# Three direct hidden tiles instead of four in a hybrid decoder layer, and low weight halves made by adding transfers

## The chip, the cores and the metric

The kernel runs on one core of a Trainium2 chip. The metric is the device time of one execution in microseconds, the median of several runs. The core's engines each work through their own list of instructions in order: TensorE (PE, matmuls), VectorE (DVE), ScalarE (ACT), GpSimd (POOL) and SyncE (SP). They wait for one another through semaphores. Transfers are issued by an engine and then run by the DMA engines.

## The reference, cut to what matters

One decoder layer on x of 512 tokens and 1024 channels, all in float32: a feed-forward network (FFN1), a mixing stage of attention, convolution and memory attention, and a second feed-forward network (FFN2).

```
D_MODEL = 1024
SEQ = 512
D_FF = 256 * math.ceil(8 * D_MODEL / 3 / 256)      # 2816
...
def rms_norm(x, g):
    xf = x.astype(jnp.float32)
    y = xf * lax.rsqrt(jnp.mean(xf * xf, axis=-1, keepdims=True) + EPS)
    return (y * g.astype(jnp.float32)).astype(x.dtype)
...
def swiglu(x, w_gate, w_up, w_down):
    return (jax.nn.silu(x @ w_gate) * (x @ w_up)) @ w_down
...
        x = x + 0.5 * swiglu(rms_norm(x, g_ffn1[l]), w_ffn1_gate[l], w_ffn1_up[l], w_ffn1_down[l])
...
        x = x + jnp.concatenate([y_attn, y_conv, y_mem], axis=-1) @ w_out[l]

        x = x + 0.5 * swiglu(rms_norm(x, g_ffn2[l]), w_ffn2_gate[l], w_ffn2_up[l], w_ffn2_down[l])
```

## The kernel before

Tokens lie along the free axis (512 columns) and channels on the partitions, so x is 8 tiles of 128x512 in SBUF. Every operand of a matmul is split in two: a high half, which is the value cast to the type fp32r, and a low half, the value minus its high half. A product is then three matmuls, high by high, high by low and low by high (`mm3`, lines 350 to 352).

**A feed-forward network** has 22 hidden tiles f of 128 channels. The first four (`N_DIRECT`) are direct: gate and up are each 8 products of 512 columns, 48 matmuls for the tile. Their matmuls read xh and xl, the split x times the gain; the factor of the norm (rb, one number per token, spread over the partitions at line 395) is multiplied in afterwards by VectorE (`evac`, lines 413 to 417). The other 18 tiles are fast (`fast`): a block scheme with seven block products in place of eight, each 4 x 3 matmuls of 256 columns (lines 447 to 449), 84 for the tile. The fast tiles need x with the factor already in it and its block sums; `blocks(k)` makes these for channel tiles k and k + 4 (lines 426 to 440), on VectorE and ScalarE. There are four calls of it, one after each direct tile but the first, and one with tile 0's evacuation. `hidden` (lines 405 and 406) splits a finished hidden tile into hh and hl.

The down projection runs in rounds over groups of hidden tiles (`ROUNDS`): each round adds its share to all eight output tiles d of x. Round 0 stands directly after the direct tiles. In it, ScalarE copies the first four outputs from PSUM with the factor 0.5 and GpSimd adds them into x by an adding transfer (lines 505 and 506); VectorE adds the others (line 509). Later rounds are mixed in among the fast tiles, one load of weights at a time. The last round feeds what follows: `nxt.add` sums the squares of x for the next norm and `scaled_split` makes the next xh and xl.

**Weights** go through one list (`Weights`): SyncE loads raw float32 weights into four raw buffers, ScalarE casts the high half (line 170) and VectorE subtracts the low half (line 171). High and low lie in one of four weight buffers, taken in rotation, so the cast for an item waits until TensorE has read the item four places earlier; and a load waits until the raw buffer four places earlier has been read. Loads run three items ahead, conversions three items ahead.

**Order.** The order of instructions on each engine is arranged by a scheduler when the kernel is built, within what the tiles allow. On TensorE FFN2's first tile stands right behind the last matmuls of the mixing stage, which read the last weights of `wout_c` (their rows are named yh and yl).

Of the kernel before, what the change touches and what calls it, by code (L numbers as in the profile page):

```python
# [30 lines left out]
F32 = mybir.dt.float32  # L31
# [3 lines left out]
AF = mybir.ActivationFunctionType  # L35
ALU = mybir.AluOpType
# [4 lines left out]
KT = 8  # L41
NF = 22
# [31 lines left out]
TILES = [s[1:] for s in ORDER if s[0] == "p"]  # L74

ON_DVE = [(0,), (1, 3), (1, 3), (2, 3), (1, 3), (1, 3)]
ROUNDS = [(0, 4), (4, 8), (8, 12), (12, 16), (16, 18), (18, 22)]
N_DIRECT = 4
WIDE, HALF, OTHER, TURNED = 64, 140, 128, 244
N_ACT = 20  # L80

# [5 lines left out]
class Weights:  # L87
# [5 lines left out]
    def __init__(self, nc, pool, dma_ahead, conv_ahead, bufs):  # L93
        self.nc, self.pool = nc, pool
        self.dma_ahead, self.conv_ahead, self.bufs = dma_ahead, conv_ahead, bufs
        self.loads, self.items = [], []
        self.raw, self.after, self.split, self.piece = {}, {}, {}, {}
        self.sums = {}
        self.extra = None
        self.by_hand = 2  # L100
        self.loaded = self.done = self.at = self.turn = 0

    def add(self, ap, off=WIDE):

        self.loads.append(ap)
        i = len(self.loads) - 1
        self.items.append((i, int(np.prod(ap.shape[1:])), off, lambda: self.raw[i]))
# [13 lines left out]
    def make_sums(self, i):  # L121
# [8 lines left out]
        nc.vector.tensor_tensor(s43[:, r], g[:, l], u[:, l], op=ALU.add)  # L130
        self.sums[i] = (s12, s43)

    def load_to(self, n):
        while self.loaded < min(n, len(self.loads)):
            i = self.loaded
            ap = self.loads[i]
            raw = self.pool.tile([P, 1024], F32, tag="wraw", name=f"wraw{i}", bufs=self.bufs[0])
            self.raw[i] = raw
            if i >= self.by_hand:
                to = raw[:, : int(np.prod(ap.shape[1:]))]  # L140
                if len(ap.shape) == 3:
                    to = to.rearrange("p (a b) -> p a b", a=ap.shape[1])
                self.nc.sync.dma_start(to, ap)
            self.loaded += 1

    def split_to(self, n):
        nc = self.nc
        while self.done < min(n, len(self.items)):
            i = self.done
            need, cols, off, src = self.items[i]  # L150
            self.load_to(need + 1)
            if need in self.after:
                self.after.pop(need)()
            if off is None:
                c = (HALF - 128) // 4
                hi, lo = (
                    self.extra.tile([P, cols + 64], F32R, tag=t, name=f"{t}{i}", bufs=1)[:, c : c + cols] for t in ("vhi", "vlo")
                )
            else:

                j = self.turn % self.bufs[1]
                c = off // 4
                self.turn += 1
                both = self.pool.tile([P, 2048 + 64], F32R, tag=f"w{j}", name=f"w{i}", bufs=1)
                hi, lo = both[:, c : c + 1024], both[:, c + 1024 : c + 2048]
            if i < self.by_hand:
                self.piece[i] = (src(), hi, lo)
            else:
                raw = src()
                nc.scalar.copy(hi[:, :cols], raw[:, :cols])  # L170
                nc.vector.tensor_tensor(lo[:, :cols], raw[:, :cols], hi[:, :cols].bitcast(F32), op=ALU.subtract)  # L171
            self.split[i] = (hi, lo)
            self.done += 1
            if i >= self.by_hand:
                self.load_to(need + 1 + self.dma_ahead)
# [9 lines left out]
    def next(self):  # L185
        i = self.at
        self.at += 1
        self.split_to(i + 1 + self.conv_ahead)
        return self.split.pop(i)


def per_load(r):

    return 8 // (ROUNDS[r][1] - ROUNDS[r][0])


def steps(f):

    r = next(r for r, (lo, hi) in enumerate(ROUNDS) if lo <= f < hi)
    if r == 0:  # L200
        return [], [], []
    m = KT // per_load(0)
    if r == 1:
        i = f - ROUNDS[1][0]
        return [(0, g) for g in range(m - 1)] if i == 0 else [], [(0, m - 1)] if i == 1 else [], []

    queue = [(q, g) for q in range(1, len(ROUNDS) - 1) for g in range(KT // per_load(q))]
    return [], [queue[f - ROUNDS[2][0]]], []


def layer(tc, ctx, a):
    nc = tc.nc
    PE, ACT, DVE, POOL = nc.tensor, nc.scalar, nc.vector, nc.gpsimd
# [28 lines left out]
    W = Weights(nc, wpool, dma_ahead=3, conv_ahead=3, bufs=(4, 4))  # L242

    def flat(w):
        return w.rearrange("p k m -> p (k m)")

    def ffn_weights(n, memory):
        gu = a[f"wgu{n}"]

        def down(r, g):  # L250
            lo, hi = ROUNDS[r]
            m = per_load(r)
            return a[f"wd{n}"][g * m : (g + 1) * m, :, lo:hi].rearrange("d p k m -> p d (k m)")

        for f in range(NF):
            pre, mid, post = steps(f)
            for d in pre:
                W.add(down(*d), OTHER if d[0] else WIDE)
            if f < N_DIRECT:
                W.add(flat(gu[f, 0]))  # L260
                W.add(flat(gu[f, 1]))
            else:
                W.add_pair(flat(gu[f, 0]), flat(gu[f, 1]), [(down(*d), OTHER if d[0] else WIDE) for d in mid])
            for d in post:
                W.add(down(*d), OTHER if d[0] else WIDE)
            if memory and f == MEM_F:
                for t in range(2):
                    W.add(flat(a["wmk"][t]), HALF)
                for c in range(2):
                    W.add(flat(a["wmv"][:, 4 * c : 4 * c + 4]), TURNED)  # L270
        r = len(ROUNDS) - 1
        for g in range(KT // per_load(r)):
            W.add(down(r, g), (HALF, OTHER)[g % 2])
# [48 lines left out]
    rb = keep.tile([P, T], F32, name="rb")  # L322
# [41 lines left out]
    class Norm:  # L364
# [5 lines left out]
        def add(self, d, engine=POOL):  # L370
            sq = work() if d else tmp.tile([P, T], F32, tag="sqsum", name=nm("sqsum"), bufs=1)
            ACT.activation(sq, x[:, d], AF.Square)
            if d == 0:
                self.sum = sq
            else:
                (engine if d < KT - 1 else DVE).tensor_tensor(self.sum, self.sum, sq, op=ALU.add)
# [13 lines left out]
        def spread(self):  # L390
            ps = tp_bank()
            for b in range(NB):
                s = slice(b * P, (b + 1) * P)
                PE.transpose(ps[:, s], self.bc[:, s], ident)
            DVE.tensor_copy(rb, ps)

    def ffn(pool, norm, first, gain, hooks, next_gain, last):
        h_hi = [None] * NF
# [4 lines left out]
        def hidden(f, t):  # L403
            h_hi[f], h_lo[f] = atile("hh"), atile("hl")
            ACT.copy(h_hi[f], t)
            DVE.tensor_tensor(h_lo[f], t, h_hi[f].bitcast(F32), op=ALU.subtract)  # L406
# [113 lines left out]
        raw = {}  # L520
        for f in range(NF):
            pre, mid, post = steps(f)
            for d in pre:
                for step in down(*d):
                    step()
            if f >= N_DIRECT:
                fast(f, mid)
            else:
                g, u = (sc_bank(), sc_bank()) if f % 3 == 2 else (mm_bank(), mm_bank())
                gh, gl = W.next()  # L530
                if f == 0:
                    uh, ul = W.next()
                    for ks in first:
                        mm3(g, gh, gl, ks, xhk, xlk, ks[0] == 0, ks[-1] == 7)
                        mm3(u, uh, ul, ks, xhk, xlk, ks[0] == 0, ks[-1] == 7)
                    norm.stats()
                    held = (g, u)
                else:
                    mm3(g, gh, gl, range(8), xhk, xlk, True, True)
                    if f == 1:  # L540
                        norm.spread()
                        raw[0] = evac(0, *held)
                        blocks(0)
                        hidden(0, raw[0])
                    uh, ul = W.next()
                    mm3(u, uh, ul, range(8), xhk, xlk, True, True)
                    raw[f] = evac(f, g, u)
                    if f == 1:
                        hidden(1, raw[1])
                    blocks(f)  # L550
                if f == N_DIRECT - 1:
                    for i in range(2, N_DIRECT):
                        hidden(i, raw[i])
            for d in post:
                for step in down(*d):
                    step()
            for hook in hooks.get(f, ()):
                hook()
# [679 lines left out]
```

## Time and profile before

| what | value |
| --- | --- |
| median of 3 runs | 864.02 us (863.29 to 864.94) |
| the profiled execution's own time | 864.32 us |
| its span in the profile | 861.8 us |
| TensorE clock granted, mean | 0.998 |
| VectorE, 512 columns, line 417 | 684 ns each |
| VectorE, subtraction of 1024 columns, line 171 | 1224 ns each |
| ScalarE, cast of 1024 columns, line 170 | 1048 ns each |
| GpSimd's issue of an adding transfer, line 506 | 864 ns in the middle, 859 to 1211 |

The table's durations are those of single instructions; on one engine the next instruction can start before the last one's tail has ended, so the steps from start to start are a little shorter. A row of the timeline has the start in us, the duration in us, engine, line, operation, what it writes and reads (without buffer numbers), shape, and in brackets how long the engine had been idle and what ended that.

### The profile page before, as it was taken

To read this page: it belongs to the slowest core of one execution; us is meant where nothing else is said; L and a number is where in the kernel's file an instruction comes from. 1 tells how busy PE (TensorE), PEld (TensorE's weight loads), DVE (VectorE), ACT (ScalarE), POOL (GpSimd) and SP (SyncE) were. 2 spreads that over 40 slices of the span, in tenths; PEclk is the share of its full clock that TensorE was granted. 3 is DMA by queue.
4 is the path that set the end of the run, shared out by engine and by line. 5 is a ranking of instruction groups with operands and counts; after the bars stand their busy time and mean duration, and the time that the engine had idled before them with its cause. 6 is when DMAs were issued, how large, how long until landed. Compare 5 with 4: busy or idle time off the path is not lost.

```text
span 861.8 us, 15658 instructions
## 1 busy us (share of the span) xinstructions
PE 854.5 (99%) x6361; PEld 790.9 (92%) x6361; DVE 696.6 (81%) x1163; ACT 445.9 (52%) x741; POOL 27.4 (3%) x30
## 2 busy tenths in 40 slices
PE   8999999999999999999999999999999999999998
PEld 5889999999999999988776888889999999999998
DVE  7998987777868797869988985998887868687772
ACT  7455555455644454533948763454654545545540
POOL 0010000000000000300000021010000000000000
PEclk9999999999999999999999999999999999999999
DMA  7335334243553334222010322335334343333312
GB/s 274 122 97 152 100 101 129 86 127 119 141 163 104 122 110 129 82 90 62 19 43 14 116 93 93 102 87 159 99 98 124 98 123 95 109 92 115 107 49 99
DMA packets 34808, 91.44 MB, mean 106 GB/s; under 512 B 3248, under 2 KB 5808, under 8 KB 34736
## 3 DMA queue, kind: packets, MB, share of 16 engines
q1 hardware_dynamic: 32000, 85.99, 32.0%
q0 software_dynamic: 1584, 2.88, 2.0%
q10 hardware_dynamic: 1152, 1.57, 0.6%
q8 instruction: 50, 0.82, 0.4%
q14 instruction: 22, 0.18, 0.1%
HBM read 85.45 MB, written 2.10 MB: 102 GB/s over the span
## 4 chain that ended last, share of the span: by engine, by line
PE 97%; DVE 1%; ACT 1%; DMA 1%; issue 0%; SPq 0%; ACTq 0%; DVEq 0%
PE mm L350 16%; PE mm L352 15%; PE mm L351 15%; PE mm L449 11%; PE mm L448 11%; PE mm L447 11%; PE sc L449 2%; PE sc L448 2%; PE sc L447 2%; PE tp L951 1%; PE sc L352 1%; PE sc L350 1%; PE sc L351 1%; PE sc L880 1%; PE tp L965 1%; PE mm L880 1%
## 5 line engine op out<-in xcount | busy, mean ns | idle before, releaser
L447 PE MATMUL mm<-bh,w 128*128 128x256 f32 x864 | 238.8, 276 | 0.0
L448 PE MATMUL mm<-bl,w 128*128 128x256 f32 x864 | 238.6, 276 | 0.0
L449 PE MATMUL mm<-bh,w 128*128 128x256 f32 x864 | 238.6, 276 | 0.0
L351 PE MATMUL mm<-hl,w 128*128 128x256 f32 (+1 forms) x640 | 183.7, 288 | 0.0
L352 PE MATMUL mm<-hh,w 128*128 128x256 f32 (+1 forms) x640 | 183.6, 287 | 0.0
L350 PE MATMUL mm<-hh,w 128*128 128x256 f32 (+1 forms) x640 | 183.1, 287 | 0.0
L170 ACT CAST w<-wraw 128x1024 fp32r<-128x1024 f32 (+2 forms) x122 | 124.0, 1020 | 86.1 <-PE mm L352 25.1
L171 DVE TENSOR_TENSOR w<-wraw,w 128x1024 fp32r<-128x1024 f32 (+2 forms) x122 | 144.5, 1189 | 28.4 <-ACT w L170 23.1
L447 PEld LDWEIGHTS mm<-bh,w 128*128 128x128 f32 x864 | 162.2, 188 | 0.2
L448 PEld LDWEIGHTS mm<-bl,w 128*128 128x128 f32 x864 | 162.2, 188 | 0.1
L449 PEld LDWEIGHTS mm<-bh,w 128*128 128x128 f32 x864 | 162.2, 188 | 0.0
L351 PEld LDWEIGHTS mm<-hl,w 128*128 128x128 f32 x640 | 120.1, 188 | 2.6 <-DVE hl L406 0.2
L352 PEld LDWEIGHTS mm<-hh,w 128*128 128x128 f32 x640 | 120.2, 188 | 2.5
L350 PEld LDWEIGHTS mm<-hh,w 128*128 128x128 f32 x640 | 120.1, 188 | 2.4
L171 DVE TENSOR_TENSOR w<-s,w 128x1024 fp32r<-128x1024 f32 x72 | 88.0, 1223 | 41.5 <-PE mm L449 34.6
L170 ACT CAST w<-s 128x1024 fp32r<-128x1024 f32 x72 | 75.7, 1051 | 24.8 <-PE mm L449 20.4
L350 PE MATMUL mm<-xh,w 128*128 128x512 f32 x192 | 75.8, 399 | 0.6 <-ACT w L182 0.6
L351 PE MATMUL mm<-xl,w 128*128 128x512 f32 x192 | 75.6, 394 | 0.6 <-DVE xl L362 0.5
L352 PE MATMUL mm<-xh,w 128*128 128x512 f32 x192 | 75.3, 392 | 0.0
L509 DVE SCALAR_TENSOR_TENSOR x<-mm,x 128x512 f32<-128x512 f32 x80 | 54.0, 683 | 1.8 <-PE mm L352 1.8
L468 ACT ACTIVATE t<-t 128x512 f32<-128x512 f32 x36 | 22.8, 633 | 61.7 <-DVE t L467 61.7
L127 DVE TENSOR_TENSOR s<-wraw 128x512 f32<-128x512 f32 x36 | 24.9, 691 | 28.8 <-DMA wraw<-in_wgu 28.6
(244 smaller groups left out, 1370.5 us busy)
## 6 DMA issues: line engine op xcount, KB each, us to landing
wraw<-in_wgu SPq DMA_DIRECT2D x86, 512.0 KB, 3.6
wraw<-in_wd SPq DMA_DIRECT2D x44, 512.0 KB, 3.6
wraw<-in_win SPq DMA_DIRECT2D x12, 512.0 KB, 3.5
x<-t POOLq DMA_DIRECT2D x8, 256.0 KB, 4.5
out<-t SPq DMA_DIRECT2D x7, 256.0 KB, 2.0
x<-in_xT SPq DMA_DIRECT2D x3, 512.0 KB, 6.3
wraw<-in_wout_a SPq DMA_DIRECT2D x6, 256.0 KB, 2.6
wraw<-in_wgu SPq DMA_DIRECT2D x4, 256.0 KB, 4.7
```

What stands on the lines that cost most here:

```text
L127: nc.vector.tensor_tensor(s12[:, l], u[:, l], u[:, r], op=ALU.add)
L170: nc.scalar.copy(hi[:, :cols], raw[:, :cols])
L171: nc.vector.tensor_tensor(lo[:, :cols], raw[:, :cols], hi[:, :cols].bitcast(F32), op=ALU.subtract)
L350: PE.matmul(ps[:, t], wh[:, w], hi(k)[:, t], start=one, stop=False, skip_group_check=cut > 1)
L351: PE.matmul(ps[:, t], wh[:, w], lo(k)[:, t], start=False, stop=False, skip_group_check=cut > 1)
L352: PE.matmul(ps[:, t], wl[:, w], hi(k)[:, t], start=False, stop=end, skip_group_check=cut > 1)
L447: PE.matmul(ps, wh[:, c], bh[k][:, block], start=one, stop=False, skip_group_check=not first)
L448: PE.matmul(ps, wh[:, c], bl[k][:, block], start=False, stop=False, skip_group_check=not first)
L449: PE.matmul(ps, wl[:, c], bh[k][:, block], start=False, stop=end, skip_group_check=not first)
L468: ACT.activation(g, g, AF.Silu)
L509: DVE.scalar_tensor_tensor(o, ps, 0.5, xd, op0=ALU.mult, op1=ALU.add)
L880: PE.matmul(banks[h][:, i * ML + c.start : i * ML + c.stop], self.q[rows, n * P : (n + 1) * P], self.kt[rows, ks], start=True, stop=True, ...
```

## The change

Direct tiles are three instead of four in both networks, and the rounds become groups of 3, 4, 4, 4, 4 and 3 hidden tiles. Round 0 now has four loads of 768 columns (two outputs with three tiles each), all listed ahead of the first fast tile; the middle rounds have one load more than there are fast tiles to take them, and it comes behind the last one. The fourth call of `blocks` stands with the third direct tile. `hidden` follows each direct tile at once. ScalarE, no longer VectorE, copies the factor rb.

Some weights, marked `by_queue`, get their low half in another way: ScalarE writes the negated high half into the place of the low half, and GpSimd then issues an adding transfer which reads the same weights from HBM once more and adds them there. So marked are tile 2 in FFN1, tiles 0, 1 and 2 in FFN2 (gate and up each), and round 0's four loads in both: 16 transfers. VectorE's subtraction is left out for these.

```diff
-ROUNDS = [(0, 4), (4, 8), (8, 12), (12, 16), (16, 18), (18, 22)]
-N_DIRECT = 4
+ROUNDS = [(0, 3), (3, 7), (7, 11), (11, 15), (15, 19), (19, 22)]
+N_DIRECT = 3
...
-    def add(self, ap, off=WIDE):
-
+    def add(self, ap, off=WIDE, by_queue=False):
+
+        if by_queue:
+            self.by_queue.add(len(self.items))
...
+    @staticmethod
+    def shaped(to, ap):
+        to = to[:, : int(np.prod(ap.shape[1:]))]
+        return to.rearrange("p (a b) -> p a b", a=ap.shape[1]) if len(ap.shape) == 3 else to
...
                 raw = src()
                 nc.scalar.copy(hi[:, :cols], raw[:, :cols])
-                nc.vector.tensor_tensor(lo[:, :cols], raw[:, :cols], hi[:, :cols].bitcast(F32), op=ALU.subtract)
+                if i in self.by_queue:
+                    nc.scalar.activation(lo[:, :cols], hi[:, :cols].bitcast(F32), AF.Copy, scale=-1.0)
+                    nc.gpsimd.dma_start(self.shaped(lo, self.loads[need]), self.loads[need], accum_op=ALU.add)
+                else:
+                    nc.vector.tensor_tensor(lo[:, :cols], raw[:, :cols], hi[:, :cols].bitcast(F32), op=ALU.subtract)
...
-    m = KT // per_load(0)
     if r == 1:
-        i = f - ROUNDS[1][0]
-        return [(0, g) for g in range(m - 1)] if i == 0 else [], [(0, m - 1)] if i == 1 else [], []
+        return [(0, g) for g in range(KT // per_load(0))] if f == N_DIRECT else [], [], []
 
     queue = [(q, g) for q in range(1, len(ROUNDS) - 1) for g in range(KT // per_load(q))]
-    return [], [queue[f - ROUNDS[2][0]]], []
+    i = f - ROUNDS[2][0]
+    return [], [queue[i]], queue[i + 1 :] if f == NF - 1 else []
...
             for d in pre:
-                W.add(down(*d), OTHER if d[0] else WIDE)
+                W.add(down(*d), OTHER if d[0] else WIDE, d[0] == 0)
             if f < N_DIRECT:
-                W.add(flat(gu[f, 0]))
-                W.add(flat(gu[f, 1]))
+                for i in range(2):
+                    W.add(flat(gu[f, i]), WIDE, n == 2 or f > 1)
...
-            DVE.tensor_copy(rb, ps)
+            ACT.copy(rb, ps)
...
                     raw[f] = evac(f, g, u)
-                    if f == 1:
-                        hidden(1, raw[1])
+                    hidden(f, raw[f])
                     blocks(f)
                 if f == N_DIRECT - 1:
-                    for i in range(2, N_DIRECT):
-                        hidden(i, raw[i])
+                    blocks(f + 1)
```

The change moves instructions on all engines. Line numbers of the changed kernel are eight higher here (350 is 358, 395 is 403).

**VectorE at the norm's factor in FFN1.** w is a weight buffer, rb the factor, t and kept the two factors of tile 0's evacuation, braw the first blocks. Before:

```order
L386 COPY t_276<-rtok 128x512
L171 TENSOR_TENSOR w_339<-wraw_201,w_339 128x1024
L395 COPY rb<-tp_309 128x512
L413 TENSOR_TENSOR t_315<-mm_196,rb 128x512
L416 TENSOR_TENSOR kept_318<-mm_197,rb 128x512
```

In the changed kernel:

```order
L394 COPY t_277<-rtok 128x512
L421 TENSOR_TENSOR t_317<-mm_196,rb 128x512
L424 TENSOR_TENSOR kept_320<-mm_197,rb 128x512
L434 SCALAR_TENSOR_TENSOR braw_323<-x,par,rb 128x512
L425 TENSOR_TENSOR kept_320<-kept_320,t_317 128x512
```

The subtraction for a weight and the copy of rb are gone from VectorE, and the evacuation follows directly.

**TensorE at the start of round 0 in FFN1.** hh and hl are the split hidden tiles in the order of their numbers, mm the outputs, the third operand the weights of round 0. Before, with tiles 0, 1 and 2 (335, 374, 549) ahead of tile 3:

```order
L352 MATMUL mm_471<-xh_155,w_393 128x512
L350 MATMUL mm_562<-hh_335,w_422 128x512
L351 MATMUL mm_562<-hl_336,w_422 128x512
L352 MATMUL mm_562<-hh_335,w_422 128x512
L350 MATMUL mm_562<-hh_374,w_422 128x512
L351 MATMUL mm_562<-hl_375,w_422 128x512
L352 MATMUL mm_562<-hh_374,w_422 128x512
L350 MATMUL mm_562<-hh_549,w_422 128x512
```

In the changed kernel, at the end of the third bank's first part (tiles 0, 1 and 2 are 337, 377 and 462):

```order
L360 MATMUL mm_529<-hh_377,w_396 128x512
L358 MATMUL mm_498<-hh_462,w_341 128x512
L358 MATMUL mm_511<-hh_462,w_341 128x512
L358 MATMUL mm_529<-hh_462,w_396 128x512
L358 MATMUL mm_542<-hh_337,w_396 128x512
L359 MATMUL mm_542<-hl_338,w_396 128x512
L359 MATMUL mm_498<-hl_463,w_341 128x512
```

Three banks (498, 511 and 529) take their six matmuls of tiles 0 and 1 first, 18 in all, and then hh of tile 2; hl of tile 2 is read five matmuls after hh.

**ScalarE at the start of FFN2.** t is a square for the norm, xh the high half of x. Before, with w_5903 for tile 1's up weights and w_5822 for tile 0's:

```order
L372 ACTIVATE t_5852<-x 128x512
L361 ACTIVATE xh_5855<-x,par 128x512
L170 CAST w_5903<-wraw_5736 128x1024
L170 CAST w_5822<-wraw_5677 128x1024
L372 ACTIVATE t_5890<-x 128x512
L361 ACTIVATE xh_5893<-x,par 128x512
```

In the changed kernel (w_6002 for tile 1, w_5919 for tile 0):

```order
L380 ACTIVATE t_5950<-x 128x512
L369 ACTIVATE xh_5953<-x,par 128x512
L175 CAST w_6002<-wraw_5833 128x1024
L177 ACTIVATE w_6002<-w_6002 128x1024
L175 CAST w_5919<-wraw_5773 128x1024
L380 ACTIVATE t_5989<-x 128x512
L177 ACTIVATE w_5919<-w_5919 128x1024
L369 ACTIVATE xh_5992<-x,par 128x512
```

A negated copy (line 177) now stands behind each cast, and a square stands between the cast of w_5919 and its negated copy. On GpSimd the transfers follow in the same order, tile 1's ahead of tile 0's.

**TensorE at the same place.** mm_5901 and mm_5902 are gate and up of tile 0 before, and mm_5983 is the gate of tile 1. Before:

```order
L352 MATMUL mm_5901<-xh_5893,w_5733 128x512
L350 MATMUL mm_5902<-xh_5893,w_5822 128x512
L351 MATMUL mm_5902<-xl_5894,w_5822 128x512
L352 MATMUL mm_5902<-xh_5893,w_5822 128x512
L381 MATMUL tp_5961<-ones,sqsum_5745 128x1 x4
L350 MATMUL mm_5983<-xh_5747,w_5860 128x512
```

In the changed kernel (gate mm_6000 and up mm_6001 of tile 0, gate mm_6084 of tile 1):

```order
L358 MATMUL mm_6001<-xh_5844,w_5919 128x512
L359 MATMUL mm_6001<-xl_5845,w_5919 128x512
L358 MATMUL mm_6000<-xh_5992,w_5829 128x512
L359 MATMUL mm_6000<-xl_5993,w_5829 128x512
L360 MATMUL mm_6000<-xh_5992,w_5829 128x512
L389 MATMUL tp_6062<-ones,sqsum_5842 128x1 x4
L358 MATMUL mm_6084<-xh_5844,w_5958 128x512
L359 MATMUL mm_6084<-xl_5845,w_5958 128x512
L360 MATMUL mm_6084<-xh_5844,w_5958 128x512
L358 MATMUL mm_6084<-xh_5858,w_5958 128x512
L360 MATMUL mm_6001<-xh_5844,w_5919 128x512
L358 MATMUL mm_6001<-xh_5858,w_5919 128x512
```

The first 21 matmuls of tile 0's gate stand ahead of these rows. The statistics (line 389) and four matmuls of tile 1 are now ahead of the first matmul that reads the low half of w_5919 (line 360), and the other 21 matmuls of tile 0's up product stand behind it.

More of the change, by code (lines that the diff above doesn't have):

```diff
@@ L98, in __init__ @@
         self.sums = {}
+        self.by_queue = set()
         self.extra = None
@@ L139, in load_to @@
             if i >= self.by_hand:
[L140 to L143, printed above, removed]
+                self.nc.sync.dma_start(self.shaped(raw, ap), ap)
             self.loaded += 1
```

## The prediction, made before the changed kernel had run

> **What bounds the kernel now.** I read the page's busy times and its chain first, then what TensorE (PE) waits for, then single stretches of the timeline (start, duration, engine, line, operation, tiles).
>
> ```profile
> span 861.8 us, 15658 instructions
> PE 854.5 (99%) x6361; PEld 790.9 (92%) x6361; DVE 696.6 (81%) x1163; ACT 445.9 (52%) x741; POOL 27.4 (3%) x30
> ...
> PE 97%; DVE 1%; ACT 1%; DMA 1%; issue 0%; SPq 0%; ACTq 0%; DVEq 0%
> ```
>
> TensorE is busy for 854.5 of 861.8 us and holds 97% of the chain that ended last. So the time falls by what TensorE no longer computes, and rises by every wait that is put in front of it; VectorE (81%) and ScalarE (52%) count only where something of theirs comes late.
>
> ```profile
> PE tp L305 <- DVE pair L318: 1.2, 1, 1.2
> PE mm L350 <- ACT w L182: 0.6, 1, 0.6
> PE mm L351 <- DVE xl L362: 0.5, 1, 0.5
> ```
>
> These are TensorE's waits of the first 100 us (total, times, longest): 2.3 us, all in the opening, and none at a hidden tile. There is hardly any wait that an edit could remove.
>
> **Part 1: two hidden tiles go from direct to fast, one in each FFN.** In the rows L350 to L352 are the three matmuls of a product, and L447 is the first of the three in a fast tile.
>
> ```profile
> 42.01 0.39 PE L350 MATMUL mm<-xh,w 128*128 128x512 f32 x1
> ...
> 52.89 0.39 PE L350 MATMUL mm<-hh,w 128*128 128x512 f32 x1
> ...
> 69.28 0.28 PE L447 MATMUL mm<-bh,w 128*128 128x256 f32 x1
> ...
> 75.75 0.28 PE L447 MATMUL mm<-bh,w 128*128 128x256 f32 x1
> ```
>
> The first two rows bound the direct tile 3: 48 matmuls in 52.89 - 42.01 = 10.88 us, 0.2267 each. The last two lie 57 matmuls of 256 columns apart in a fast tile: 6.47 us, 0.1135 each; its 84 take 9.53. The difference is 1.35 us a tile, **-2.70 us** for two. The down products only change rounds: their number stays, and one of 512 columns (0.2267) costs what two of 256 do (0.2270).
>
> **Part 2: does VectorE keep up with an earlier round 0?** In FFN1 round 0 now starts at 42.01, after three direct tiles.
>
> ```profile
> 12.00:58.00 46.00, 45.52 (x206) 37.25 (x205) 43.95 (x73) 25.87 (x34) 0.00 (x0) 1.00 0.42 142
> ...
> 25.42 1.05 ACT L170 CAST w<-wraw 128x1024 fp32r<-128x1024 f32 x1 [3.94 <-DVE t L386]
> ...
> 26.50 1.23 DVE L171 TENSOR_TENSOR w<-wraw,w 128x1024 fp32r<-128x1024 f32 x1 [1.09 <-ACT w L170]
> 27.64 0.68 DVE L395 COPY rb<-tp 128x512 f32<-128x512 f32 x1
> 28.36 0.69 DVE L413 TENSOR_TENSOR t<-mm,rb 128x512 f32<-128x512 f32 x1
> 28.97 0.68 DVE L416 TENSOR_TENSOR kept<-mm,rb 128x512 f32<-128x512 f32 x1
> 29.57 0.74 DVE L426 SCALAR_TENSOR_TENSOR braw<-x,par,rb 128x512 f32<-128x512 f32 x1
> ```
>
> The first row has TensorE, its weight loads, VectorE and ScalarE busy in this stretch: VectorE 43.95 of 46.00, ScalarE 25.87. So VectorE is the tight one, and the change takes from it the copy of the factor rb and the subtractions for tile 2 and round 0, while ScalarE takes on a copy and the negated copies. In the rows, rb's copy stood behind the subtraction at 26.50, which waited for its cast. Copied by ScalarE it should be ready near 27.5, not 28.36.
>
> From there to the evacuation of tile 2's second product, VectorE has 26 instructions in the new order. I price them by steps from start to start: 0.60 for an operation on 512 columns (28.36 to 28.97 to 29.57) and 1.14 for 1024 (26.50 to 27.64), so about 1.07 for each further 1000 columns. By that line 256 columns are 0.335 and 768 are 0.87; a scalar_tensor_tensor (0.74 against 0.68) gets 0.66. 12 x 0.60 + 6 x 0.66 + 4 x 0.335 + 2 x 0.87 + 2 x 1.14 = 16.5, so that evacuation starts at 44.0. Two more steps and ScalarE's cast (0.62) give hh of tile 2 at 46.5. TensorE begins round 0 with the 18 matmuls of three banks that need only tiles 0 and 1: 42.01 + 18 x 0.2267 = 46.09. I take a wait of **+0.5**; the low half hl, used five matmuls later, comes at 47.7 and adds next to nothing. The least is 0. The most is 1.2: a cast for the first fast tile stands ahead of hh of tile 1 on ScalarE and waits for its load, worth 0.7 if that comes late. FFN2 copies rb with more slack, as its statistics move ahead of the second half of tile 0; there I take 0. The casts and subtractions for the first fast tile end by this ledger 0.5 to 2.8 us ahead of their matmuls (near 58.8), which is no cost but no comfort.
>
> **Part 3: the adding transfers.** There are 16 new ones: 6 in FFN1, 10 in FFN2. Each waits for a cast and a negated copy on ScalarE, then reads the weights from HBM a second time. The trace has adding transfers, of half the size.
>
> ```profile
> x<-t POOLq DMA_DIRECT2D x8, 256.0 KB, 4.5
> mtot<-t POOLq DMA_DIRECT2D x3, 256.0 KB, 5.2
> ...
> wraw<-in_wgu SPq DMA_DIRECT2D x86, 512.0 KB, 3.6
> ...
> DMA to landing us min/median/max: 3.4/4.5/7.8
> ...
> q1 hardware_dynamic: 32000, 85.99, 32.0%
> q0 software_dynamic: 1584, 2.88, 2.0%
> ```
>
> Eleven transfers of 256 KB make up q0: 0.020 x 861.8 / 11 = 1.57 us of all 16 DMA engines each. On q1 a MB takes 0.32 x 861.8 / 85.99 = 3.2 us, so 256 KB take 0.8: adding costs about twice a plain load. The bottom row of landing times is that of the eight into x: 3.4 at least, 4.5 in the middle, 7.8 at most. A second 256 KB adds 1.57: I estimate 5.0, 6.1 and 9.4 us for 512 KB. The lowest bound is 3.6, what a plain load of that size takes.
>
> ```profile
> 19.48 2.00 ACT L170 CAST w<-wraw 128x1024 fp32r<-128x1024 f32 x2 [1.23 <-PE mm L352]
> ...
> 31.13 0.39 PE L350 MATMUL sc<-xh,w 128*128 128x512 f32 x1
> ...
> 509.25 1.03 ACT L170 CAST w<-wraw 128x1024 fp32r<-128x1024 f32 x1
> ```
>
> Where there is lead, this hides. In FFN1 the pair of casts at 19.48 is tile 2's; the gate's negated copy follows, and its transfer issues near 22.4 to land from 27.4 to 31.8, where TensorE wants it two matmuls into tile 2, at 31.6. The last piece of round 0 can be cast when tile 2 ends (42.01), issues near 43.9, lands by 53.3 at worst, and is wanted two matmuls into the seventh of eight outputs: 42.01 + 0.5 + 56 x 0.2267 = 55.2. FFN2's gate weights for tile 0 are cast at 509.25, issue near 512 and are wanted two matmuls after 522.36, beyond the 9.4. What TensorE computes meanwhile is the cover.
>
> **The place without lead is FFN2's first up weights.** Their buffer is the one from which the last matmuls of the mixing stage read.
>
> ```profile
> 522.13 0.39 PE L352 MATMUL mm<-yh,w 128*128 128x512 f32 x1
> 522.36 0.39 PE L350 MATMUL mm<-xh,w 128*128 128x512 f32 x1
> ...
> 533.24 0.95 PE L381 MATMUL tp<-ones,sqsum 128*128 128x1 f32 x8
> 534.05 0.49 PE L350 MATMUL mm<-xh,w 128*128 128x512 f32 x1
> ...
> 521.02 0.71 ACT L361 ACTIVATE xh<-x,par 128x512 fp32r<-128x512 f32 x1
> 521.64 1.98 ACT L170 CAST w<-wraw 128x1024 fp32r<-128x1024 f32 x2
> 524.94 0.64 ACT L372 ACTIVATE t<-x 128x512 f32<-128x512 f32 x1 [1.32 <-DVE x L1132]
> 525.48 0.71 ACT L361 ACTIVATE xh<-x,par 128x512 fp32r<-128x512 f32 x1
> ...
> 523.03 1.21 DVE L171 TENSOR_TENSOR w<-wraw,w 128x1024 fp32r<-128x1024 f32 x1
> 524.17 0.68 DVE L1132 TENSOR_TENSOR x<-mm,x 128x512 f32<-128x512 f32 x1
> 524.77 1.21 DVE L171 TENSOR_TENSOR w<-wraw,w 128x1024 fp32r<-128x1024 f32 x1
> ```
>
> Mixing's last matmul starts at 522.13 and ends near 522.5. Before, ScalarE cast both the second tile's and these weights from 521.64 on, and VectorE had the low half at 526, in good time. Now the same half goes this way: the second tile's cast and negated copy hold ScalarE until 523.55 (521.64 + 2 x 0.95, since two took 1.98 with the last one's tail); the cast of w_5919 runs to 524.5, a square to 525.0 (0.53, from 524.94 to 525.48), its negated copy to 526.0; then GpSimd issues the transfer, near 526.0. No row has a negated copy; I price it as a cast of the same size, and even at half of that the landing moves by half a microsecond. Before the first matmul that reads this half TensorE has 26 matmuls of tile 0, the statistics (534.05 - 533.24 = 0.81) and 4 matmuls of tile 1: 522.36 + 30 x 0.2267 + 0.81 = 529.97. All later work of TensorE stands behind it, and nothing else can go ahead.
>
> Landing, and so the wait: with 3.6 us 529.6, no wait; with 5.0, 531.0 and 1.0; with 6.1, 532.1 and 2.1; with 9.4, 535.4 and 5.4. This one is not alone: tile 1's adding transfer of 512 KB was issued 2.4 us ahead on the same queue, and the cast of w_5919 frees the raw buffer for which three weight loads (512, 384 and 384 KB, by the rate above 4 us of all engines) stand in SyncE's queue, just then. All three transfers together are 2 x 3.14 + 4.0 = 10.3 us of work from about 525 on: 535.3 if this half is the very last of it, 531.3 if the loads yield. I take the middle, landing near 533.4: **+3.4 us**, from 0 to 5.4.
>
> A rule speaks against that. The Trainium skill, "DMA: Bandwidth & Descriptors", section "Anatomy of one DMA — SWDGE (gpsimd) path", fits a GpSimd transfer as 2.0 us plus its bytes over 436e3 per us, an estimate of 3.2 us for 512 KB: landing at 529.2, no wait, and a sum of 861.8. The same fit gives 2.6 us for 256 KB, which took 3.4 to 7.8 here, so the trace does not agree.
>
> **Sum.** -2.70 + 0.5 + 3.4 = +1.2. The profiled execution took 864.32 us (span 861.8 and 2.5 around it), 0.30 above the median of 864.02; it becomes 865.5, the median **865.2**. Within 0.2% (1.73 us, about what a measurement of this kernel tells from no change) means 862.3 to 865.75.
>
> **Rivals.**
> - The transfer lands in time. For it speak the fast plain loads (3.6 us for the size). Against it: the least of eight adding transfers of half the size took 3.4. Then only -2.70 + 0.5 remains: 861.8, faster; without the half microsecond at round 0, 861.3.
> - Slower: the transfer into w_5919 gets its turn last behind the three loads and tile 1's transfer, 9.4 us or more. It decides from a wait of 3.9 us on, that is a landing after 533.9. The price at 5.4 is 864.02 - 2.70 + 0.5 + 5.4 = 867.2. For it: 7.8 us did occur for 256 KB, and here two transfers share a queue. Against it: the middle of eight was 4.5.
> - VectorE's chain is later than the ledger: its stretch was 96% busy and the first fast tile has margins from 0.5 us. Two us more in FFN1 give 865.2 + 2.0 = 867.2.
> - The change does not do what it says (fast tiles save nothing): 865.2 + 2.7 = 867.9. The spacing rows speak clearly against it.
>
> **How the numbers follow.** Forecast, a wait from 0.5 to 3.9 us: 0.42. In time: 0.24. Late: 0.24. VectorE: 0.08. No saving: 0.02, slower too. So faster 0.24, same 0.42, slower 0.34. The range goes from 861.3 (no waits) to 864.02 - 2.70 + 1.2 + 5.4 = 867.9. It leaves out what lies beyond 9.4 us in the late case, and the end of VectorE's.
>
> **What would show it.** Right: fast tiles at 9.53 us, TensorE's span of work 2.7 us shorter, a wait of about half a microsecond for hh at 46, and one of about 3 us at the third matmul of tile 0's up product near 530, released by a transfer. If that wait is absent, my landing times are wrong and the time is below 862.3. If waits stand at the first fast tile instead, my VectorE ledger is wrong. If fast tiles are spaced wider than 0.1135 us per matmul, the saving is.

## The result, and the profile after

| kernel | median | ratio to before, 95% interval |
| --- | --- | --- |
| before | 863.85 us (6 runs) | |
| changed | 869.34 us (6 runs) | 1.0068, 1.0056 to 1.0079 |

The change makes the kernel slower by 5.5 us. The prediction was 865.2 with a range from 861.3 to 867.9, so the time lies above its upper end. The profiled execution of the changed kernel took 869.31 us, with a span of 867.5, 5.7 longer than before. One of the ten executions of e1 below took 4868 us: e1's median counts it (864.20 without it), its ratio does not.

The page of the changed kernel, its span, busy times, chain and two queues:

```profile
span 867.5 us, 15976 instructions
...
PE 853.1 (98%) x6481; PEld 793.8 (92%) x6481; DVE 686.9 (79%) x1160; ACT 466.7 (54%) x776; POOL 46.0 (5%) x46
...
q1 hardware_dynamic: 32064, 85.99, 31.8%
q0 software_dynamic: 4912, 10.23, 7.3%
...
PE 81%; DVE 9%; ACT 4%; DMA 3%; issue 3%; SPq 0%; POOL 0%; DVEq 0%; ACTq 0%; POOLq 0%
```

TensorE still bounds the kernel, but its share of the chain fell from 97% to 81%: VectorE, ScalarE and the DMA engines have come into it. q0, the adding transfers, went from 2.88 to 10.23 MB. At 0.073 x 867.5 / 10.23 = 6.2 us a MB it takes twice what q1 does (0.318 x 867.5 / 85.99 = 3.2), as the prediction had it.

TensorE's waits in the changed kernel (total us, times, longest):

```profile
PE mm L360 <- DMA w<-in_wgu: 3.3, 1, 3.3
PE mm L455 <- ACT kept L470: 1.5, 2, 0.8
PE mm L359 <- DVE xl L370: 1.2, 2, 0.7
PE tp L313 <- DVE pair L326: 1.2, 1, 1.2
PE mm L358 <- ACT hh L413: 1.1, 1, 1.1
PE mm L358 <- DVE s L904: 1.0, 1, 1.0
PE mm L358 <- ACT xh L369: 0.7, 1, 0.7
```

The three largest new ones are the adding transfer at FFN2's start (3.3), ScalarE's evacuation of fast tiles (1.5, in each network once) and hh at round 0 (1.1); xl has 0.7 more than before and xh 0.7. With the small ones not shown all waits sum to 10.8 us, 6.8 more than the 4.0 of before. -2.7 for the saved matmuls and +6.8 give +4.1; the span grew by 5.7. Part of the rest is in the next view.

The timeline of TensorE in the changed kernel at the place that the prediction called decisive:

```profile
530.48 0.40 PE L358 MATMUL mm<-xh,w 128*128 128x512 f32 x1
534.19 0.78 PE L360 MATMUL mm<-xh,w 128*128 128x512 f32 x1 [3.31 <-DMA w<-in_wgu]
534.77 0.63 PE L358 MATMUL mm<-xh,w 128*128 128x512 f32 x1
...
537.33 0.55 PE L358 MATMUL mm<-xh,w 128*128 128x512 f32 x1
537.72 0.39 PE L359 MATMUL mm<-xl,w 128*128 128x512 f32 x1
537.95 0.40 PE L360 MATMUL mm<-xh,w 128*128 128x512 f32 x1
```

The third matmul of the up product waits 3.31 us for the transfer. But the eight matmuls from 534.19 to 537.72 then stand some 0.43 us apart and not 0.227: 3.53 us for what takes 1.81, another 1.7 us. The windows of the same kernel (TensorE, its loads, VectorE, ScalarE, GpSimd busy; then the granted clock, the DMA share and GB/s) show why:

```profile
530.00:534.00 4.00, 0.88 (x4) 0.38 (x2) 2.12 (x13) 1.19 (x2) 1.04 (x1) 1.00 1.06 255
534.00:536.00 2.00, 1.81 (x4) 1.47 (x5) 0.00 (x0) 0.00 (x0) 0.00 (x0) 0.56 0.96 168
536.00:538.00 2.00, 2.00 (x7) 1.56 (x6) 0.00 (x0) 0.00 (x0) 0.00 (x0) 0.58 0.65 129
538.00:540.00 2.00, 2.00 (x10) 1.64 (x9) 0.00 (x0) 0.00 (x0) 0.00 (x0) 1.00 0.00 0
```

The granted clock is 0.56 and 0.58 in the two windows after the wait, and 1.00 again after that. At half speed that is (0.44 + 0.42) x 2 / 0.5 = 3.4 us. The mean over the run, 0.998, hides it. It is 0.998 before as well, because that profiled execution has a slow stretch of its own, in the mixing stage:

```profile
454.00:456.00 2.00, 2.00 (x14) 1.42 (x15) 1.80 (x11) 2.00 (x8) 0.00 (x0) 0.84 0.04 8
456.00:458.00 2.00, 2.00 (x10) 1.27 (x8) 1.26 (x12) 1.51 (x6) 0.00 (x0) 0.50 0.52 133
458.00:460.00 2.00, 2.00 (x14) 1.40 (x13) 2.00 (x12) 1.53 (x5) 0.00 (x0) 0.81 0.01 2
```

TensorE takes 10.77 us there (449.18 to 459.95) for what takes 9.49 in the changed kernel (451.00 to 460.49), whose clock is 1.00 in the mixing stage.

So -2.7 + 6.8 + 1.7 = +5.8 comes near the 5.7, but in part by luck. The 1.3 us of the slow stretch before are missing in this sum. On the other side the listed waits are too short by up to 0.3 us each: from 530.48 to 534.19 it is 3.71 us, 3.48 more than a step, where 3.31 is listed. The two errors roughly cancel.

### The profile page after: what moved, and what is told of

Same layout as the page of the kernel before. It is cut to its first block, busy times and chain, and to the rows that moved or that the text cites. A ratio compares the mean times of both kernels' runs of the same rounds, so it can differ in the third digit from the quotient of the medians.

```text
span 867.5 us, 15976 instructions
## 1 busy us (share of the span) xinstructions
PE 853.1 (98%) x6481; PEld 793.8 (92%) x6481; DVE 686.9 (79%) x1160; ACT 466.7 (54%) x776; POOL 46.0 (5%) x46
## 3 DMA queue, kind: packets, MB, share of 16 engines
q1 hardware_dynamic: 32064, 85.99, 31.8%
q0 software_dynamic: 4912, 10.23, 7.3%
## 4 chain that ended last, share of the span: by engine, by line
PE 81%; DVE 9%; ACT 4%; DMA 3%; issue 3%; SPq 0%; POOL 0%; DVEq 0%; ACTq 0%; POOLq 0%
PE mm L358 13%; PE mm L360 13%; PE mm L359 13%; PE mm L455 10%; PE mm L457 10%; PE mm L456 10%; DVE w L180 2%; PE sc L457 2%; PE sc L456 2%; PE sc L455 2%; DMA wraw<-in_wgu 2%; PE tp L957 1%; ACT p L922 1%; DMA w<-in_wgu 1%; PE sc L359 1%
## 5 line engine op out<-in xcount | busy, mean ns | idle before, releaser
L455 PE MATMUL mm<-bh,w 128*128 128x256 f32 x912 | 252.3, 277 | 1.5 <-ACT kept L470 1.5
L456 PE MATMUL mm<-bl,w 128*128 128x256 f32 x912 | 251.9, 276 | 0.0
L457 PE MATMUL mm<-bh,w 128*128 128x256 f32 x912 | 251.9, 276 | 0.0
L358 PE MATMUL mm<-hh,w 128*128 128x256 f32 (+1 forms) x656 | 185.7, 285 | 1.1 <-ACT hh L413 1.1
L360 PE MATMUL mm<-hh,w 128*128 128x256 f32 (+1 forms) x656 | 186.2, 284 | 0.0
L455 PEld LDWEIGHTS mm<-bh,w 128*128 128x128 f32 x912 | 171.2, 188 | 1.9 <-ACT kept L470 1.9
L456 PEld LDWEIGHTS mm<-bl,w 128*128 128x128 f32 x912 | 171.2, 188 | 0.1
L457 PEld LDWEIGHTS mm<-bh,w 128*128 128x128 f32 x912 | 171.2, 188 | 0.0
L180 DVE TENSOR_TENSOR w<-wraw,w 128x1024 fp32r<-128x1024 f32 (+2 forms) x108 | 125.2, 1161 | 34.7 <-ACT w L175 32.8
L358 PEld LDWEIGHTS mm<-hh,w 128*128 128x128 f32 x656 | 123.1, 188 | 3.3 <-ACT hh L413 1.5
L360 PEld LDWEIGHTS mm<-hh,w 128*128 128x128 f32 x656 | 123.1, 188 | 1.8
L360 PE MATMUL mm<-xh,w 128*128 128x512 f32 x160 | 63.8, 398 | 3.3 <-DMA w<-in_wgu 3.3
L358 PE MATMUL mm<-xh,w 128*128 128x512 f32 x160 | 64.0, 405 | 1.0 <-ACT xh L369 0.7
L359 PE MATMUL mm<-xl,w 128*128 128x512 f32 x160 | 63.7, 398 | 1.3 <-DVE xl L370 1.2
L175 ACT CAST vhi<-wraw 128x512 fp32r<-128x512 f32 x38 | 23.6, 621 | 48.1 <-PE sc L456 42.6
```

The source lines that it names most:

```text
L358: PE.matmul(ps[:, t], wh[:, w], hi(k)[:, t], start=one, stop=False, skip_group_check=cut > 1)
L359: PE.matmul(ps[:, t], wh[:, w], lo(k)[:, t], start=False, stop=False, skip_group_check=cut > 1)
L360: PE.matmul(ps[:, t], wl[:, w], hi(k)[:, t], start=False, stop=end, skip_group_check=cut > 1)
L455: PE.matmul(ps, wh[:, c], bh[k][:, block], start=one, stop=False, skip_group_check=not first)
L456: PE.matmul(ps, wh[:, c], bl[k][:, block], start=False, stop=False, skip_group_check=not first)
L457: PE.matmul(ps, wl[:, c], bh[k][:, block], start=False, stop=end, skip_group_check=not first)
```

## Experiments

All are timed against the kernel before. "Wait" is TensorE's, from the profile.

**e1: FFN2's tile 0 back to VectorE.**

```diff
-                    W.add(flat(gu[f, i]), WIDE, n == 2 or f > 1)
+                    W.add(flat(gu[f, i]), WIDE, f > (0 if n == 2 else 1))
```

> FFN2's tile 0 gets its low halves from VectorE again, all else as in the changed kernel. Theory (the late adding transfer into tile 0's up weights costs its 3.5 us of waiting and, on top, the 1.7 us of half-speed matmuls that follow it): both go, about 869.3 - 5.2 = 864.1 us, and no wait of over 1 us between 520 and 545. Rival (VectorE has no room there, so a subtraction comes late in place of the transfer): a wait <-DVE of 2 us or more near 530, 866 or above.

Measured: 864.38 us, ratio 1.0007 (0.9996 to 1.0017). There is no wait over 0.2 us between 500 and 610, and no slow matmul. So FFN2's tile 0 accounts for 5.0 of the 5.5 us, and VectorE had room for its subtractions. What remains undoes the saving: waits of 1.6 us for hh at FFN1's round 0 and of 1.7 us in all at fast tiles.

**e2: tile 0 by transfer, tile 1 not.**

```diff
-                    W.add(flat(gu[f, i]), WIDE, n == 2 or f > 1)
+                    W.add(flat(gu[f, i]), WIDE, f != 1 if n == 2 else f > 1)
```

> In FFN2 tile 1 is taken out of the adding transfers, tile 0 stays in. ScalarE is then free a microsecond earlier for tile 0's up weights and no transfer stands ahead in the queue. I expect the transfer to issue near 525 and a wait of 0 to 1.5 us. Theory (the slow matmuls come from the clock falling after an idle of over 3 us): with so short a wait no matmul is slow, 864.2 to 865.8 us. Rival (the matmuls are slow because the adding transfers disturb them): 6 to 8 matmuls of 0.43 us remain after the transfer, about 1.7 us more.

Measured: 868.82 us, 1.006 (1.0043 to 1.0077). My expectation failed twice. The wait was 2.7 us: the transfer landed 2.6 us earlier than in the changed kernel, but in the new order the statistics and tile 1's four matmuls stood behind the up product, so it was wanted some 2 us earlier too. And an idle of 2.7 us was long enough for the clock. e2's windows, the wait and what follows:

```profile
528.70:531.60 2.90, 0.19 (x1) 0.00 (x0) 0.00 (x0) 2.10 (x2) 0.24 (x1) 1.00 0.89 164
531.60:535.20 3.60, 3.57 (x9) 2.81 (x10) 0.00 (x0) 0.00 (x0) 0.61 (x1) 0.53 0.92 184
535.20:538.00 2.80, 2.80 (x14) 2.32 (x13) 0.00 (x0) 0.00 (x0) 0.00 (x0) 1.00 0.39 75
```

Here the DMA engines are busy throughout (0.92), so e2 alone does not tell idle from traffic. e4 and e10 do.

**e3: no adding transfers for weights.**

```diff
-                W.add(down(*d), OTHER if d[0] else WIDE, d[0] == 0)
+                W.add(down(*d), OTHER if d[0] else WIDE)
...
-                    W.add(flat(gu[f, i]), WIDE, n == 2 or f > 1)
+                    W.add(flat(gu[f, i]), WIDE)
```

> No adding transfers for weights at all: three direct tiles, the new rounds and rb by ScalarE remain, VectorE subtracts all low halves. Theory (the transfers relieve VectorE in FFN1, where it is the tight engine, and are a loss in FFN2 only): the 5.2 us in FFN2 go, and the wait for hh of tile 2 in FFN1 grows from 1.2 us to 3 or 4, since two subtractions of 1.14 us come ahead of it; 865.5 to 867.5 us. Rival (VectorE has room, the transfers were never needed): the wait at round 0 stays at 1.2 us or less, 863 to 864.

Measured: 867.65 us, 1.0044 (1.0029 to 1.0058), just above what the theory gave, and with the waits in another place. e3's longest wait:

```profile
PE mm L455 <- DVE x L517: 4.2, 2, 2.1
```

hh of tile 2 is in time without a transfer. VectorE's subtractions for round 0 instead delay its additions into x, which free the banks that the first fast tile needs: 2.1 us in each network. So the transfers do relieve VectorE, in FFN2 as well, which I had not expected. In FFN1 it is round 0's that count, since e6 has only these and no such wait; in FFN2 no run separates them from those of tiles 1 and 2. After this idle the clock stayed: e3's next window in FFN1, with matmuls at full pace, is

```profile
62.00:64.00 2.00, 2.00 (x20) 2.00 (x20) 2.00 (x4) 0.37 (x1) 0.00 (x0) 1.00 0.38 154
```

That is the profiled execution. Two of e3's five executions had a lower mean clock (0.998 and 0.996 against 1.000) and took 1 to 2 us longer, so idles of 2.1 us are not shown to be safe.

**e4: round 0's fourth load listed inside the second fast tile.**

```diff
-        return [(0, g) for g in range(KT // per_load(0))] if f == N_DIRECT else [], [], []
+        m = KT // per_load(0)
+        return [(0, g) for g in range(m - 1)] if f == N_DIRECT else [], [(0, m - 1)] if f == N_DIRECT + 1 else [], []
```

> Round 0's fourth load is listed inside the second fast tile, as before the change; all else as in the changed kernel. Theory (the fifth fast tile waits 0.8 and 1.0 us for ScalarE's evacuation because nearly five fast tiles in a row carry no down product, and VectorE with the loads cannot keep their pace of 9.5 us): the 2.2 us of down work in between give VectorE time, both waits shrink or go, 867.3 to 868.3 us. Rival (the waits have another cause, as a late load): they stay, 869 or above.

Measured: 874.75 us, 1.0125 (1.011 to 1.014), the worst of all and a miss. The fast tiles' waits did shrink, to 0.4 us each (the load between them carries 18 matmuls, 4.1 us of down work and not 2.2). FFN2's wait of 3.3 us stayed. And the first fast tile's weights moved up one place in the list, and with them their cast on ScalarE. e4's ScalarE:

```profile
35.18 0.62 ACT L175 CAST vhi<-wraw 128x512 fp32r<-128x512 f32 x1 [4.56 <-DMA wraw<-in_wgu]
35.71 0.83 ACT L443 CAST bh<-braw 128x768 fp32r<-128x768 f32 x1
36.44 0.63 ACT L423 ACTIVATE t<-t 128x512 f32<-128x512 f32 x1
```

The cast waits 4.56 us for its load, and what VectorE needs for blocks and hidden tiles stands behind it. hh of tile 2 then comes 4.1 us late. Nothing of this has to do with FFN2, yet the matmuls after it are slow as well. e4's windows there:

```profile
47.00:51.00 4.00, 0.00 (x0) 0.00 (x0) 4.00 (x7) 2.52 (x4) 0.00 (x0) 1.00 0.55 92
51.00:52.50 1.50, 1.45 (x4) 1.17 (x5) 1.50 (x4) 0.00 (x0) 0.00 (x0) 0.67 0.00 0
52.50:55.00 2.50, 2.50 (x7) 1.95 (x6) 2.50 (x4) 1.96 (x3) 0.02 (x1) 0.52 0.00 0
```

The clock is at 0.52 while the DMA engines do nothing (0.00) and the wait was for ScalarE. So matmuls are slow behind an idle in another place too, with no traffic beside them.

**e6: e1, and FFN1's tile 2 back to VectorE.**

```diff
-                    W.add(flat(gu[f, i]), WIDE, n == 2 or f > 1)
+                    W.add(flat(gu[f, i]), WIDE, n == 2 and f > 0)
```

> On top of e1 (FFN2's tile 0 by VectorE), FFN1's tile 2 gets its low halves from VectorE too, which is idle there during the factor's steps; FFN1's only adding transfers are then round 0's. Theory (the wait for hh of tile 2 in FFN1, 1.2 to 1.8 us, comes from a load for the first fast tile that is issued only at 32.8 and then takes 5.2 us, ahead of hh on ScalarE): the load is issued no earlier without tile 2's transfers, so the wait stays over 1 us and the time at 864.0 to 864.8. Rival (tile 2's transfers at 23.4 delay all that follows): the wait falls below 0.5 us, 862.8 to 863.4.

Measured: 863.26 us, 0.9993 (0.9984 to 1.0002). The rival was right in its number. In the chain of the changed kernel and of e6 the load for the first fast tile is

```profile
32.81 5.24 DMA wraw<-in_wgu
```

```profile
33.88 3.70 DMA wraw<-in_wgu
```

It starts later in e6, as my theory said it would be no earlier, but it takes 3.7 us and not 5.2. In e6 the wait for hh in FFN1 is no longer among those that the profile lists (the one of 0.3 us is FFN2's).

The wait follows this load. The changed kernel, e1, e2 and e7 have the same code up to there, and yet ScalarE's wait for the load was 3.04, 3.64, 2.74 and 2.35 us in their profiles, and TensorE's for hh 1.1, 1.6, 0.7 and 0.3. Without tile 2's transfers, in e6 and e8, ScalarE waited 1.44 and 1.30 us and TensorE not at all. That these transfers slow the load is what the difference suggests; how much of it is theirs is not shown, with a spread of 1.3 us between equal codes.

**e7: e1, and rounds of 3, 3, 4, 4, 4, 4.**

```diff
-ROUNDS = [(0, 3), (3, 7), (7, 11), (11, 15), (15, 19), (19, 22)]
+ROUNDS = [(0, 3), (3, 6), (6, 10), (10, 14), (14, 18), (18, 22)]
```

> On top of e1, the rounds are 3, 3, 4, 4, 4, 4 in place of 3, 4, 4, 4, 4, 3: down work goes in among the fast tiles from the fourth of them on, not the fifth. Theory (the waits of 1.0 us in each network at the fifth fast tile come from VectorE, which is busy without a break behind round 0 and falls behind the fast tiles' 9.5 us until down work gives it time): both waits shrink by at least half, 862.4 to 863.4 us. Rival (these waits hang on a late load, not on the pace): they stay at 1 us, 864 to 865.

Measured: 861.87 us, 0.9981 (0.9972 to 0.999), a little better than expected: the fastest of all, and faster than the kernel before. First the changed kernel's windows behind round 0, with VectorE busy as the third pair of numbers:

```profile
60.00:70.00 10.00, 10.00 (x89) 9.92 (x87) 9.97 (x14) 5.90 (x10) 0.00 (x0) 1.00 0.41 126
70.00:79.00 9.00, 9.00 (x82) 9.00 (x81) 9.00 (x13) 5.61 (x10) 0.00 (x0) 1.00 0.37 118
79.00:88.50 9.50, 9.50 (x86) 9.50 (x86) 9.50 (x15) 5.48 (x10) 0.00 (x0) 1.00 0.38 112
```

VectorE works without a break for three tiles while TensorE still runs at its pace; the lag reaches TensorE only at 104.7, and by way of a load. The chain and VectorE's timeline in the changed kernel have

```profile
92.26 4.25 DMA wraw<-in_wgu
```

```profile
96.53 0.69 DVE L130 TENSOR_TENSOR s<-wraw 128x512 f32<-128x512 f32 x1 [1.72 <-DMA wraw<-in_wgu]
```

In the chain this load starts when a subtraction of VectorE ends (92.24), which reads a raw buffer, and VectorE then has to idle 1.72 us for it. FFN2's chain has the same load, 4.26 us from 610.70 on, ahead of the wait there. So theory and rival each name a part: a load is late because VectorE is. From there on VectorE is behind again:

```profile
103.74 0.62 ACT L413 CAST hh<-t 128x512 fp32r<-128x512 f32 x1 [1.09 <-DVE t L490]
104.26 0.38 ACT L470 ACTIVATE kept<-mm 128x256 f32<-128x256 f32 x1
```

the evacuation (L470) for which TensorE waits stands on ScalarE behind a cast of the tile before, and that waits for VectorE. The stretch from 79.0 to 88.5 in e7:

```profile
79.00:88.50 9.50, 9.50 (x86) 9.50 (x86) 8.14 (x12) 6.01 (x11) 0.00 (x0) 1.00 0.35 112
```

VectorE has 1.4 us of rest there already, before the fourth fast tile with its down work begins at 88.9; the order of the weight list has changed too, and no run separates the two. e7's waits at fast tiles fell from the 1.7 us of e1 to 0.3, and its chain no longer has that load. This is not all of the 2.5 us by which e7 is faster than e1: its profile also has 1.3 us less wait for hh, in the same code, and 0.7 less for xl.

**e8: e6 and e7 together.**

```diff
-ROUNDS = [(0, 3), (3, 7), (7, 11), (11, 15), (15, 19), (19, 22)]
+ROUNDS = [(0, 3), (3, 6), (6, 10), (10, 14), (14, 18), (18, 22)]
...
-                    W.add(flat(gu[f, i]), WIDE, n == 2 or f > 1)
+                    W.add(flat(gu[f, i]), WIDE, n == 2 and f > 0)
```

> e6 and e7 together, the version with the best prospect. By e7's theory and e6's theory 862.3 to 863.6 us; if both rivals hold, about 863; faster than the kernel before by 0.1 to 0.2% at best. Waits over 0.5 us that I expect to remain: at the opening, for hh of tile 2 in FFN1, and for xl near 365.

Measured: 862.61 us, 0.9985 (0.9976 to 0.9995). Faster than before, and not to be told from e7. The waits for hh in FFN1 and for xl near 365, which I expected to remain, are not among those listed; 0.6 us at fast tiles are.

**e9: the kernel before, rb copied by ScalarE.**

```diff
-            DVE.tensor_copy(rb, ps)
+            ACT.copy(rb, ps)
```

> The kernel before with one edit: ScalarE copies the factor rb. Theory (VectorE's relief there hides behind TensorE, which waits for nothing in that stretch): no change, 863.6 to 864.6 us. Rival (an earlier factor moves the whole start): faster by 0.7 us or more in the two networks, 862.5 to 863.3.

Measured: 864.01 us, 1.0006 (0.9997 to 1.0015): no difference, as the theory had it.

**e10 and e11: the kernel before, with one adding transfer.** e10 gives FFN2's tile 0 its low up half by negated copy and transfer, e11 its low gate half. The code in `Weights` is that of the change without the helper `shaped`; besides, in e10

```diff
-                W.add(flat(gu[f, 1]))
+                W.add(flat(gu[f, 1]), WIDE, n == 2 and f == 0)
```

> The kernel before, with four direct tiles and its own rounds, and one thing added: FFN2's tile 0 gets the low half of its up weights by a negated copy and an adding transfer. Theory (this one transfer, with the idle it causes, is the loss of the changed kernel): a wait <-DMA of 1.5 to 4 us near 529; if it is over some 2.7 us, 7 or 8 matmuls of 0.43 us follow and cost 1.5 to 1.8 more, if it is under 2.2 us none do. 865.5 to 869.0 us. Rival (alone in its queue the transfer is in time, and only the changed kernel's traffic made it late): no wait over 0.5 us, 863.5 to 864.5.

and in e11

```diff
-                W.add(flat(gu[f, 0]))
+                W.add(flat(gu[f, 0]), WIDE, n == 2 and f == 0)
```

> The same with the gate weights of that tile in place of the up weights; their buffer is free some 13 us before TensorE wants them. Theory (the transfer is harmless where its buffer is free early): no wait near 523, 863.5 to 864.6 us. Rival (an adding transfer costs wherever it stands, by its traffic or by ScalarE's extra copy): 865 or above.

Measured: e10 871.52 us, 1.0083 (1.0067 to 1.01); e11 863.26 us, 0.9999 (0.9989 to 1.0008). e10's time is above what I gave, the mechanism is as the theory said; e11 is as expected. e10's timeline and a window of it:

```profile
527.19 0.39 PE L359 MATMUL mm<-xh,w 128*128 128x512 f32 x1
531.81 0.50 PE L359 MATMUL mm<-xh,w 128*128 128x512 f32 x1 [4.23 <-DMA w<-in_wgu]
...
533.21 0.63 PE L357 MATMUL mm<-xh,w 128*128 128x512 f32 x1
```

```profile
534.00:536.00 2.00, 2.00 (x6) 1.52 (x5) 0.00 (x0) 0.00 (x0) 0.00 (x0) 0.55 0.00 0
```

One transfer of 512 KB in the one place where its buffer comes free late costs a wait of 4.2 us and half speed behind it; the same transfer for the gate costs nothing. And again the clock is at 0.55 with no DMA traffic at all. e10's median lies above its profiled execution of 869.27 us: the other three took 871.2 to 872.0, with a mean granted clock of 0.994 against 0.998. By an estimate from these, 0.004 x 870 / 0.5, they had some 7 us more at half speed; where is not recorded. The two slowest executions of the changed kernel (870.20 and 871.63) have 0.995 and 0.994 likewise.

## Why the prediction was wrong, step by step

**Saved matmuls, -2.70: right.** A fast tile has its pace of before; in the changed kernel 57 matmuls of the first one take

```profile
60.35 0.28 PE L455 MATMUL mm<-bh,w 128*128 128x256 f32 x1
...
66.82 0.28 PE L455 MATMUL mm<-bh,w 128*128 128x256 f32 x1
```

6.47 us, the same as before.

**The transfer at FFN2's start, +3.4: the wait was right, its price was not.** The steps up to the issue held: ScalarE and GpSimd in the changed kernel,

```profile
521.83 1.05 ACT L175 CAST w<-wraw 128x1024 fp32r<-128x1024 f32 x1 [0.90 <-PE mm L360]
522.91 1.06 ACT L177 ACTIVATE w<-w 128x1024 fp32r<-128x1024 f32 x1
523.88 1.03 ACT L175 CAST w<-wraw 128x1024 fp32r<-128x1024 f32 x1
524.81 0.63 ACT L380 ACTIVATE t<-x 128x512 f32<-128x512 f32 x1
525.35 1.04 ACT L177 ACTIVATE w<-w 128x1024 fp32r<-128x1024 f32 x1
```

```profile
526.69 0.86 POOL L178 DMA_DIRECT2D w<-in_wgu  x1 [1.54 <-ACT w L177]
```

show the order and the lengths that I had put together; the transfer was issued at 526.7 (near 526.0 forecast, in a stretch that ran 0.6 later) and took 7.46 us in the chain, 7.4 in the forecast. All 16 transfers landed after 5.0, 6.0 and 10.3 us (least, middle, most), against 5.0, 6.1 and 9.4 estimated for 512 KB; the page gives a middle of 6.7 for the eight of 512 KB and 5.4 for the eight of 384 KB.

That 7.46 met 7.4 is partly luck. The 7.4 was the middle between 5.3 and 9.3 us, reasoned from tile 1's transfer in the same queue and three loads. In e10 no other adding transfer stood there, and the same transfer took 7.60 us from issue to landing; in e2, without tile 1's, it took 6.11, and the gate's in e11 6.2. So tile 1's transfer is not needed for such a time, and what sets it stays open.

**The step that failed is the last one, "the wait costs its length".** It cost 3.3 us and another 1.7, because TensorE's clock was at half speed behind it. Without the wait both go (e1: -5.0 us). The Trainium skill describes such a clock, in "TensorE: Matmul & The Clock Gate", section "Part 1: The HAM clock gate": after about 3.4 us without work the clock halves, and it returns after about as long at work. I did not weigh that page. The runs agree on the half speed and on how long it lasts, and show it for a shorter idle: 2.7 us did it in e2.

**VectorE at round 0, +0.5: a wait came, but not the one that was priced.** VectorE's ledger held: it began at 27.39 (27.5 forecast) and reached tile 2's evacuation at 45.32, after 17.9 us; 1.2 of them it waited for ScalarE, so its work took 16.7 (16.5 forecast). TensorE came there 0.6 later than forecast. By these numbers hh would have been just in time without the 1.2 us, as in e6 and e8. The 1.1 us measured is what the forecast had only in its bound of 1.2: the cast for the first fast tile ahead of hh of tile 1 on ScalarE waited for its load.

```profile
38.07 0.62 ACT L175 CAST vhi<-wraw 128x512 fp32r<-128x512 f32 x1 [3.04 <-DMA wraw<-in_wgu]
38.59 0.62 ACT L413 CAST hh<-kept 128x512 fp32r<-128x512 f32 x1
```

**Fast tiles, taken as 0: wrong.** My ledger ended at the first fast tile, whose inputs were in time. Four fast tiles now run without down work behind a round 0 that VectorE leaves late, and I did not follow its lag, and the load that waits for VectorE, to the fifth: 1.5 us in all. In e7, which shortens that run by a tile, 0.3 us is left.

**Small ones not forecast.** The wait for xh at the opening, 0.7 us here, is 0.2 in e1, where the code of that place is the same, so I give it no cause. Near 365, at the start of the mixing stage, the changed kernel waits 0.7 us for xl. The same wait stands in e1, e2, e3, e4 and e6, whose last round has three tiles, and in none of the kernels whose last round has four (before, e7, e8, e9, e10, e11). A shorter last round, which leaves less time for each output's xl, would explain it; no run changed that alone.

**Together.** 1.7 us for the clock, 1.5 at the fast tiles, 0.6 more at round 0 and 1.4 for xh and xl are 5.2 that the forecast did not have; the median lies 4.1 above it. The record does not close the gap of about a microsecond: executions of the kernel before take 863 to 865 us, with and without a slow stretch, and the forecast started from one with it.

**The rivals.** "Late" (867.2) had the right place, but its condition did not come: the wait was 3.3 us and not over 3.9. "VectorE is later" was right in part: its lag cost 1.5 us, at the fifth fast tile of each network and not at the first of FFN1. The range was too narrow because its upper end had neither the clock nor the fast tiles; with the 1.7 us alone it would have reached 869.6.

## What to carry to other kernels

Follow a weight's buffer back to its last reader before choosing how to fill it: a slow path (copy, transfer, landing) was free where the buffer was idle for some ten microseconds (e11), and where TensorE had just left it (e10), whatever of it TensorE's other work did not cover was waited for. On a bound TensorE here, single waits of 2.7 us and more were dearer than their length, since the matmuls behind them ran at half speed for another 3.4 us. An engine that is busy in every window of a stretch may be late already, even where nobody yet waits for it: follow it to the end of the stretch, with the loads that wait for it.

## What was not expected of the hardware

In the profiles TensorE's clock stayed at 1.00 behind the idles of 2.1 us (e3) and was at half speed behind those of 2.7 us (e2), 3.3 (changed kernel), 4.1 (e4) and 4.2 (e10). The slow stretch had the same length each time: 3.4 us by the windows (e2: 0.47 x 3.6 / 0.5). It came with the DMA engines idle (e4, e10) and busy (e2). But the listed idle is not the whole rule. The kernel before had such a stretch, 3.4 us too, at 455, with no wait of TensorE listed in the ten microseconds ahead; it had small matmuls there (16 of two columns in 1.84 us), and the same rows of the changed kernel ran at 1.00. What decides it stays open. An adding transfer of weights took about twice the DMA time of a plain load of the same size (6.2 against 3.2 us a MB).
